# A two-layer trunk on one core: on-chip last slot groups, six query tiles, diagonal weighting in the first layer

## The chip, the cores and the metric

The kernel runs on one core of one Trainium2 chip. The metric is the device time of the whole launch in microseconds (us). The engines are TensorE (PE in the profile, its weight loads PEld), VectorE (DVE), ScalarE (ACT), GpSimd (POOL) and SyncE (SP), which issues most DMAs.

## The reference, cut to what matters

Two layers over 256 latent tokens and 256 context tokens of width 1024, in float32. A layer normalises and projects its input, runs three mixers beside each other (a long convolution, a gated recurrence called gdn, and attention with eight heads), merges them, projects, adds; then a mixture of experts adds its part:

```python
qn_l, qr_l = mla_queries(cq_l, lp)        # 8 heads: 64 plain + 32 rotary columns each
qr_l = rope_2d(qr_l, row, col)            # latent tokens only
...
x = x + (gt1 * mix).astype(x.dtype)
h2 = rms_norm(x, lp['norm2_g']) * (1.0 + sc2) + sh2
x = x + (gt2 * moe_ffn(h2, router_w, router_b, lp)).astype(x.dtype)
# moe_ffn: for each token its 2 best of 16 experts,
#   gate[:, e] * ((silu(h @ w1[e]) * (h @ w3[e])) @ w2[e]), summed
...
return rms_norm(x, final_norm_g)          # after two layers, 256 latent tokens
```

The second layer updates only the latent tokens, so its experts see 256 rows in place of 512.

## The kernel before

SBUF is an arena of 47 pages of 128 x 1024 float32, handed out in halves (`M.get`). PSUM is eight banks of 128 x 512. Work is written in two forms. *Items* are a list in a fixed order: each has weight loads on SP's queue, a preparation, products, and a post step. *Streams* are generators (a recurrence, attention, an expert's activation) that a planner (`Plan`, L267) steps in between the products of the items, by clocks that it keeps for each engine. Each engine then executes in the order in which its instructions were written. Large products are made three times from high and low parts (`mm3`, L420); `split_block` (L413) makes these parts with a ScalarE cast and a VectorE subtraction.

**Queries** (`uq_item`, L1600). Eight items a layer, one for a head. An item loads 96 columns of the weight for six row blocks. `swap` (L863) then copies the 32 rotary columns once more with halves exchanged, so that the tile has 128 columns: 64 plain, 32 rotary, 32 rotary exchanged. It is split, and 18 products follow (6 blocks x 3), over 512 token columns in layer 0 and 256 in layer 1. The post step multiplies the two rotary parts by cosines and sines out of the bank, adds, and copies the rest. The first item of a layer (`abkr_item`, L838) does the same for the one rotary key.

**Experts of layer 1** (`moe_sets`, L2208). The slots are packed in twelve groups (`NSET`) of 128 rows, each made of four runs of 32 slots of one expert. Group n goes through eight up items and, one group later, four down items. After a group's last down item its two banks are copied to a page and a GpSimd indirect DMA scatters the rows into the DRAM table `yd`, two rows a token.

**After the experts.** `overflow` (L2492) loads the largest slot count and holds a branch (L2497) that all engines pass; its body runs only when an expert has more rows than slots. Then `load_y` (L2286) reads the two rows of each token back from `yd` on SP's queue. `combine` (L2295) weighs them (ScalarE, VectorE), multiplies by the gate row (GpSimd, the last one on VectorE), adds to the residual (VectorE) and squares for the norm (ScalarE). In layer 0 that works on four token tiles of 1024 columns, in layer 1 on two tiles in halves. In layer 0 the norm of layer 1 follows and the transposes that feed its first products. In layer 1 the final norm and gain follow and the two output DMAs.

Of the kernel before, what the change touches and what calls it, by code (L numbers as in the profile page):

```python
# [28 lines left out]
D = 1024  # L29
SEQ = 256  # L30
L = 2
# [11 lines left out]
def _constants():  # L43
# [27 lines left out]
    ra, rb = np.zeros((128, SEQ)), np.zeros((128, SEQ))  # L71
    ra[32:64], ra[64:96] = c32, s32
    rb[64:96], rb[96:128] = c32, s32
    cols["ropeA"], cols["ropeB"] = ra, rb
# [287 lines left out]
LAG = (2, 1)  # L362


class Trunk:
# [209 lines left out]
    def setup(self):  # L575
# [7 lines left out]
        self.yd = [self.dr.tile([1024 >> l, D], F32, name=f"yd{l}") for l in range(L)]  # L583
        self.tokd = [self.dr.tile([512 * NE, 1], I32, name=f"tokd{l}") for l in range(L)]
# [253 lines left out]
    def abkr_item(self, l):  # L838
# [8 lines left out]
        def prep0(pg):  # L847
            self.swap(pg, 32, 64, 8)

        def post(b):  # L850
            ab, kr, t2 = self.M.get(), self.M.get(), self.M.get()
            nc.scalar.copy(ab.f()[0:16], b[0:16, :])
            ra = self.c("ropeA")
            nc.vector.tensor_tensor(kr.f()[64:96, :SEQ], b[32:64, :SEQ], ra[32:64], op=OP.mult)
            nc.vector.tensor_tensor(t2.f()[64:96, :SEQ], b[64:96, :SEQ], ra[64:96], op=OP.mult)
            nc.vector.tensor_tensor(kr.f()[64:96, :SEQ], kr.f()[64:96, :SEQ], t2.f()[64:96, :SEQ], op=OP.add)
# [4 lines left out]
        return self.win(l, 0, 512, post, "abkr", loader, prep0)  # L861

    def swap(self, pg, a, b, k):  # L863

        src = pg[:, :, a:a + 32].rearrange("p k (u s c) -> p k u s c", u=2, s=2)
        dst = pg[:, :, b:b + 32].rearrange("p k (u s c) -> p k u s c", u=2, s=2)
        for u in range(2):
            for s in range(2):
                self.nc.vector.tensor_copy(dst[:, :, u, s, :], src[:, :, u, 1 - s, :])
# [730 lines left out]
    def uq_item(self, l, h):  # L1600

        nc, M = self.nc, self.M
        nt = 512 if l < L - 1 else 256
        w = self.a["mla_w_uq"][l].rearrange("(k p) c -> p k c", p=128)

        def ld(blk):
            nc.sync.dma_start(out=blk.f(768).rearrange("p (k c) -> p k c", k=6)[:, :, 0:96], in_=w[:, :, 96 * h:96 * h + 96])

        def prep(it):
            p = it.pages[0]  # L1610
            self.swap(p.f(768).rearrange("p (k c) -> p k c", k=6), 64, 96, 6)
            it.w = self.split_block(p, 768)

        def mm(it):
# [8 lines left out]
            if h == 7:  # L1623
                for hi, lo in self.lora["q"]["x"]:
                    hi.free()
                    lo.free()

        def post(it):
            b = it.b
            q, t = M.get(), M.get()  # L1630
            rb = self.c("ropeB")
            nc.scalar.copy(q.f(nt)[0:64], b[0:64, :nt])
            nc.vector.tensor_tensor(q.f(SEQ)[64:96], b[64:96, :SEQ], rb[64:96], op=OP.mult)
            nc.vector.tensor_tensor(t.f(SEQ)[64:96], b[96:128, :SEQ], rb[96:128], op=OP.mult)
            nc.vector.tensor_tensor(q.f(SEQ)[64:96], q.f(SEQ)[64:96], t.f(SEQ)[64:96], op=OP.add)
            if nt > SEQ:
                nc.scalar.copy(q.f()[64:96, SEQ:], b[64:96, SEQ:nt])
            t.free()
            self.unbank(b)
            self.qt[h] = q  # L1640
        return Item([(2, ld)], prep, mm, post, name=f"uq{h}")
# [566 lines left out]
    def moe_sets(self, l):  # L2208
# [17 lines left out]
        def up(n, j, q):  # L2226
# [24 lines left out]
        def down(n, k):  # L2251
# [14 lines left out]
            def post(it):  # L2266
# [3 lines left out]
                y = M.get(2)  # L2270
                for hf, b in enumerate(st.pop((n, "y"))):
# [4 lines left out]
                y.free()  # L2276
            return Item([(2, ld(e)) for e in new(n)], None, mm, post, name=f"down{n}{k}", need=(f"act{n}",), moe=True)
# [6 lines left out]
        return items  # L2284

# [9 lines left out]
    def combine(self, tiles, ys, parts, after):  # L2295
# [3 lines left out]
        n = D // parts  # L2299
        units = [(t, n * i) for t in tiles for i in range(parts)]  # L2300
        ss = self.tiny(8, "css")

        def weigh(u, t, o):
            y0, y1 = ys[t, 0].f(n, o), ys[t, 1].f(n, o)
            nc.scalar.activation(y0, y0, AF.Copy, scale=self.gw[0][:, t:t + 1])
            v.scalar_tensor_tensor(y0, y1, self.gw[1][:, t:t + 1], y0, op0=OP.mult, op1=OP.add)

        def gate(u, t, o):
            y0 = ys[t, 0].f(n, o)
            (v if u == len(units) - 1 else nc.gpsimd).tensor_tensor(y0, y0, self.gt2[t // 2].f(n, o), op=OP.mult)  # L2310

        def add(u, t, o):
            x = self.xt[t].f(n, o)
            v.tensor_tensor(x, x, ys[t, 0].f(n, o), op=OP.add)

        def square(u, t, o):
            x = self.xt[t].f(n, o)
# [284 lines left out]
```

## Time and profile before

| | |
|---|---|
| time, median of 3 runs | 2086.78 us (2080.86 to 2089.03) |
| the profiled execution, its own time | 2080.96 us |
| its span, first to last instruction | 2079.3 us |
| mean granted TensorE clock | 0.94 of full speed |
| TensorE busy | 1850.6 us |
| VectorE busy | 1300.7 us |
| ScalarE busy | 873.3 us |
| GpSimd busy | 318.5 us |

Busy time is the union of an engine's instructions in the profiled execution. All helpers record their operations at one line, L210, so rows are told apart by their tiles: `pg` is a page, `bank` a PSUM bank, `cst` a constant, `yd` the table of expert rows.

### The profile page before, as it was taken

To read this page: it belongs to the slowest core of one execution; us is meant where nothing else is said; L and a number is where in the kernel's file an instruction comes from. 1 tells how busy PE (TensorE), PEld (TensorE's weight loads), DVE (VectorE), ACT (ScalarE), POOL (GpSimd) and SP (SyncE) were. 2 spreads that over 40 slices of the span, in tenths; PEclk is the share of its full clock that TensorE was granted. 3 is DMA by queue.
4 is the path that set the end of the run, shared out by engine and by line. 5 is a ranking of instruction groups with operands and counts; after the bars stand their busy time and mean duration, and the time that the engine had idled before them with its cause. 6 is when DMAs were issued, how large, how long until landed. Compare 5 with 4: busy or idle time off the path is not lost. (4 is left out here: it accounts for less than half of the span.)

```text
span 2079.3 us, 32681 instructions
## 1 busy us (share of the span) xinstructions
PE 1850.6 (89%) x12412; PEld 1369.9 (66%) x12413; DVE 1300.7 (63%) x2799; ACT 873.3 (42%) x1520; POOL 318.5 (15%) x314
## 2 busy tenths in 40 slices
PE   4899998899999989699999488998989977899993
PEld 1776786677768777588888366787768966233331
DVE  2667566654675669799999676777777755111113
ACT  3342423444434534288888444443455432111111
POOL 2212112000032204311110201131011310100002
PEclk8999999999999999799999798999989988999997
DMA  9717212412253274689998585622415529799961
GB/s 334 256 62 218 70 38 57 111 42 82 92 182 80 85 247 162 243 326 386 380 381 314 152 282 170 174 55 57 120 31 163 143 86 391 248 394 391 385 256 70
DMA packets 295184, 401.10 MB, mean 193 GB/s; under 512 B 43892, under 2 KB 185722, under 8 KB 295016
## 3 DMA queue, kind: packets, MB, share of 16 engines
q1 hardware_dynamic: 271512, 360.38, 51.5%
q0 software_dynamic: 13056, 27.15, 3.7%
q10 hardware_dynamic: 10448, 11.37, 1.7%
q8 instruction: 100, 1.64, 0.3%
q14 instruction: 68, 0.56, 0.1%
HBM read 391.94 MB, written 23.20 MB: 200 GB/s over the span
## 5 line engine op out<-in xcount | busy, mean ns | idle before, releaser
L210 PE MATMUL bank<-pg,pg 128*128 128x512 f32 (+6 forms) x10746 | 1659.6, 390 | 57.8 <-ACT pg L210 31.3
L210 PEld LDWEIGHTS bank<-pg,pg 128*128 128x128 f32 (+4 forms) x10746 | 1212.8, 167 | 455.9 <-issue 203.9
L210 DVE TENSOR_TENSOR pg<-pg,pg 128x1024 fp32r<-128x1024 f32 (+11 forms) x699 | 608.5, 903 | 157.7 <-ACT pg L210 147.8
L210 ACT CAST pg<-pg 128x1024 fp32r<-128x1024 f32 (+3 forms) x460 | 428.8, 965 | 209.7 <-DVE pg L210 139.0
L210 ACT COPY pg<-bank 64x256 f32<-64x256 f32 (+5 forms) x402 | 163.7, 440 | 285.1 <-PE bank L210 238.0
L210 PE MATMUL bank<-cst,pg 128*128 128x128 f32 (+3 forms) x935 | 142.5, 290 | 103.7 <-DVE pg L210 64.1
L210 PEld LDWEIGHTS bank<-cst,pg 128*128 128x128 f32 (+1 forms) x935 | 118.2, 159 | 147.4 <-issue 51.6
L210 POOL TENSOR_TENSOR pg<-pg,pg 128x512 f32<-128x512 f32 (+3 forms) x72 | 119.6, 1667 | 441.2 <-DVE pg L210 196.2
L210 ACT ACTIVATE pg<-bank 128x512 f32<-128x512 f32 (+1 forms) x116 | 61.0, 535 | 166.9 <-PE bank L210 156.3
L210 ACT ACTIVATE pg<-pg 128x512 f32<-128x512 f32 (+4 forms) x77 | 52.7, 692 | 146.8 <-DVE pg L210 107.1
L210 DVE SCALAR_TENSOR_TENSOR pg<-bank,vec,pg 128x510 f32<-128x510 f32 (+3 forms) x112 | 73.5, 657 | 54.6 <-ACT pg L210 52.8
L210 DVE SCALAR_TENSOR_TENSOR pg<-pg,bank 128x512 f32<-128x512 f32 (+1 forms) x92 | 54.2, 602 | 77.2 <-ACT pg L210 64.7
L210 POOL DMA_INDIRECT yd<-pg,t_vi x28 | 29.0, 1037 | 465.3 <-ACT pg L210 235.8
L210 DVE TENSOR_TENSOR pg<-bank,pg 128x512 fp32r<-128x512 f32 (+4 forms) x120 | 69.1, 596 | 27.3 <-ACT pg L210 14.6
L210 ACT CAST pg<-bank 128x512 fp32r<-128x512 f32 (+1 forms) x72 | 35.6, 517 | 100.4 <-PE bank L210 80.2
L210 DVE TENSOR_TENSOR pg<-pg,bank 128x512 f32<-128x512 f32 (+1 forms) x44 | 27.0, 613 | 80.6 <-PE bank L210 77.8
L210 POOL TENSOR_TENSOR pg<-pg 128x512 f32<-128x512 f32 (+1 forms) x12 | 14.3, 1193 | 400.0 <-ACT pg L210 348.3
L210 ACT ACTIVATE pg<-bank,t_amx,t_asq 128x512 f32<-128x512 f32 (+1 forms) x48 | 34.0, 708 | 77.4 <-DVE t_amx L210 77.4
L210 ACT ACTIVATE pg<-bank,vec 128x512 f32<-128x512 f32 (+3 forms) x64 | 41.4, 647 | 59.5 <-PE bank L210 53.6
L210 DVE COPY pg<-bank 128x512 f32<-128x512 f32 x12 | 8.3, 692 | 82.2 <-PE bank L210 75.3
L210 PE MATMUL bank<-pg,sc 128*32 128x512 f32 x384 | 53.5, 630 | 0.8 <-DMA pg<-in_w_ada_dram 0.7
L210 DVE TENSOR_REDUCE pg<-pg 128x128 f32<-128x1024 f32 (+15 forms) x128 | 43.1, 337 | 4.4
(258 smaller groups left out, 814.0 us busy)
## 6 DMA issues: line engine op xcount, KB each, us to landing
pg<-in_moe_w_dram SPq DMA_DIRECT2D x384, 512.0 KB
pg<-in_w_in_dram SPq DMA_DIRECT2D x120, 512.0 KB
pg<-in_w_ada_dram SPq DMA_DIRECT2D x96, 512.0 KB
pg<-in_w_out_dram SPq DMA_DIRECT2D x24, 512.0 KB
pg<-yd SPq DMA_DIRECT2D x12, 512.0 KB
pg<-in_mla_w_uq_dram SPq DMA_DIRECT2D x16, 288.0 KB
pg<-gcd POOLq DMA_DIRECT2D x16, 256.0 KB, 4.1
pg<-in_hy_out_dram SPq DMA_DIRECT2D x8, 512.0 KB
```

The lines of the kernel that those rows point to most:

```text
L210: return f(*a, **k)
```

## The change

Four edits.

1. Queries come from six items a layer: four of two heads' plain columns, two of four heads' rotary columns. The exchange of halves is a VectorE shuffle within 32 partitions after the product, for the key too.
2. In layer 1 the last two slot groups are not scattered. Their rows are weighted and gated out of the banks, stay in pages, and one-hot products add them to the tokens at the end (`finish`). The other ten groups' rows are read back and added by a stream (`partial`) that starts after group 9. The table is zeroed early in the layer, since rows that stay on the chip leave places in it unwritten.
3. The weights and one-hot tables for that are made when group 3 starts (`tail_weights`).
4. In layer 0 two of the four token tiles (`DIAG`) are weighted by products with diagonal matrices, and the gate multiplication of all tiles is on VectorE.

```diff
+DIAG = (1, 3)
+TAIL = (NSET - 2, NSET - 1)
+TURN = [i ^ 8 for i in range(32)]
...
-    def uq_item(self, l, h):
+    def uq_item(self, l, kind, i):
+        n, o = (64, 0) if kind == "plain" else (32, 64)
+        heads = 128 // n
         def ld(blk):
-            nc.sync.dma_start(out=blk.f(768).rearrange("p (k c) -> p k c", k=6)[:, :, 0:96], in_=w[:, :, 96 * h:96 * h + 96])
+            pg = blk.f(768).rearrange("p (k c) -> p k c", k=6)
+            for j in range(heads):
+                c = 96 * (heads * i + j) + o
+                nc.sync.dma_start(out=pg[:, :, n * j:n * j + n], in_=w[:, :, c:c + n])
...
+        def plain(it):
+            for j in range(2):
+                nc.scalar.copy(self.qt[2 * i + j].f(nt)[0:64], it.b[64 * j:64 * j + 64, :nt])
+        def rotary(it):
+            r, t = M.get(), M.get()
+            nc.scalar.copy(r.f(nt), it.b[:, :nt])
+            x, y = t.f(SEQ), t.f(SEQ, SEQ)
+            v.stream_shuffle(y, r.f(SEQ), TURN)
+            v.tensor_tensor(x, r.f(SEQ), self.c("ropeC"), op=OP.mult)
+            v.tensor_tensor(y, y, self.c("ropeS"), op=OP.mult)
+            for j in range(4):
+                q = self.qt[4 * i + j] = M.get()
+                p = slice(32 * j, 32 * j + 32)
+                v.tensor_tensor(q.f(SEQ)[64:96], x[p], y[p], op=OP.add)
+                if nt > SEQ:
+                    nc.scalar.copy(q.f()[64:96, SEQ:], r.f(nt)[p, SEQ:])
...
+                if (n, j, q) == (3, 0, 0):
+                    self.tail_weights()
...
+                if n in TAIL:
+                    for hf, b in enumerate(st.pop((n, "y"))):
+                        nc.vector.scalar_tensor_tensor(y.f(512, 512 * hf), b, self.gws[:, n - TAIL[0]:n - TAIL[0] + 1], self.gt2[0].f(512, 512 * hf), op0=OP.mult, op1=OP.mult)
+                    self.tail[n] = y
+                    return
...
+                if n == TAIL[0] - 1:
+                    self.start("partial", self.partial(l))
...
+    def zero_rows(self, l, eng):
+        z = self.M.get(2)
+        self.nc.gpsimd.memset(z.f(), 0.0)
+        for t in range(8 >> l):
+            eng.dma_start(out=self.yd[l][128 * t:128 * t + 128], in_=z.f())
...
+    def add_rows(self, l, t, eng):
+        for i, y in enumerate((y0, y1)):
+            eng.dma_start(out=y.f(), in_=src[:, i, :])
+        yield self.plan.when(y1.f())
+        x = self.xt[t].f()
+        nc.scalar.activation(y0.f(), y0.f(), AF.Copy, scale=self.gw[0][:, t:t + 1])
+        v.scalar_tensor_tensor(y0.f(), y1.f(), self.gw[1][:, t:t + 1], y0.f(), op0=OP.mult, op1=OP.add)
+        v.tensor_tensor(y0.f(), y0.f(), self.gt2[t // 2].f(), op=OP.mult)
+        v.tensor_tensor(x, x, y0.f(), op=OP.add)
+    def partial(self, l):
+        for t in range(2):
+            yield from self.add_rows(l, t, self.nc.gpsimd)
+    def finish(self, l):
+        for hf in range(2):
+            for j, n in enumerate(TAIL):
+                for t in range(2):
+                    if j == 0:
+                        bank[t] = self.bank()
+                    nc.tensor.matmul(bank[t], self.hot.f(128, 128 * (2 * j + t)), self.tail[n].f(512, 512 * hf), start=j == 0, stop=j == len(TAIL) - 1)
+            for t in range(2):
+                x = self.xt[t].f(512, 512 * hf)
+                v.tensor_tensor(x, x, bank[t], op=OP.add)
+                nc.scalar.activation(sq.f(), x, AF.Square, accum_out=ss[:, 2 * t + hf:2 * t + hf + 1])
+        v.tensor_tensor(x0, x0, self.fg.f(), op=OP.mult)
...
+        r = self.rows_rms(self.xt[:2], "fin", s2)
+        nc.scalar.activation(x0, x0, AF.Copy, scale=r[:, 0:1])
+        nc.scalar.dma_start(out=self.out[0, 0:128], in_=x0)
+        v.scalar_tensor_tensor(x1, x1, r[:, 1:2], self.fg.f(), op0=OP.mult, op1=OP.mult)
+        nc.sync.dma_start(out=self.out[0, 128:256], in_=x1)
...
+    def combine(self, ys, after):
+        for t in DIAG:
+            for hf in range(2):
+                b = bank[t, hf] = self.bank()
+                for i in range(2):
+                    nc.tensor.matmul(b, self.dg[t].f(128, 128 * i), ys[t, i].f(512, 512 * hf), start=i == 0, stop=i == 1)
+        for t in range(4):
+            if t in DIAG:
+                for hf in range(2):
+                    v.tensor_tensor(y0.f(512, o), bank[t, hf], g.f(512, o), op=OP.mult)
+                    v.tensor_tensor(x.f(512, o), x.f(512, o), y0.f(512, o), op=OP.add)
+                    nc.scalar.activation(y1.f(512, o), x.f(512, o), AF.Square, accum_out=s8[:, 2 * t + hf:2 * t + hf + 1])
+            else:
+                nc.scalar.activation(y0.f(), y0.f(), AF.Copy, scale=self.gw[0][:, t:t + 1])
+                v.scalar_tensor_tensor(y0.f(), y1.f(), self.gw[1][:, t:t + 1], y0.f(), op0=OP.mult, op1=OP.add)
+                v.tensor_tensor(y0.f(), y0.f(), g.f(), op=OP.mult)
+                v.tensor_tensor(x.f(), x.f(), y0.f(), op=OP.add)
+                nc.scalar.activation(y1.f(), x.f(), AF.Square, accum_out=ss[:, t:t + 1])
...
         items = [self.abkr_item(l)] + ([hook(self.late_setup)] if l == 0 else []) + qkv(0)
+        items += [hook(lambda: self.zero_rows(l, nc.gpsimd))] if l == L - 1 else []
...
+            self.drain(("filters",) if l < L - 1 else ("partial",))
             if l < L - 1:
+                self.diagonals()
             self.overflow(l)
```

## Rows read from the trace of the kernel before

**Rows 1.** The page: busy time, share of the span, instructions

```profile
PE 1850.6 (89%) x12412; PEld 1369.9 (66%) x12413; DVE 1300.7 (63%) x2799; ACT 873.3 (42%) x1520; POOL 318.5 (15%) x314
```

**Rows 2.** Windows: length, busy PE PEld DVE ACT POOL, clock, DMA share, GB/s

```profile
380.00:400.00 20.00, 15.95 (x64) 11.95 (x63) 13.53 (x37) 7.70 (x13) 0.00 (x0) 0.91 0.11 27
400.00:420.00 20.00, 20.00 (x86) 15.77 (x85) 13.51 (x29) 9.62 (x18) 0.00 (x0) 1.00 0.69 184
...
1420.00:1440.00 20.00, 16.61 (x191) 15.34 (x193) 15.28 (x46) 7.53 (x17) 0.00 (x0) 0.83 0.25 62
...
2020.00:2030.00 10.00, 10.00 (x100) 3.04 (x96) 0.69 (x1) 0.60 (x1) 0.01 (x1) 1.00 0.07 24
```

**Rows 3.** Timeline, TensorE in the query stages: start, us, instruction, count

```profile
402.82 9.49 PE L210 MATMUL bank<-pg,pg 128*128 128x512 f32 x39
...
1446.82 3.42 PE L210 MATMUL bank<-pg,pg 128*128 128x256 f32 x32 [0.49 <-DVE pg L210]
```

**Rows 4.** Grouped lines, VectorE, 1400 to 1462: busy us, mean ns | idle before

```profile
L210 DVE TENSOR_TENSOR pg<-pg,pg 128x768 fp32r<-128x768 f32 x8 | 7.7, 959 | 7.5 <-ACT pg L210 7.5
L210 DVE TENSOR_TENSOR pg<-bank,cst 32x256 f32<-32x256 f32 x16 | 6.8, 425 | 3.1 <-ACT pg L210 2.8
...
L210 DVE COPY pg<-pg 128x48 f32<-128x48 f32 x32 | 4.5, 205 | 0.2
...
L210 DVE TENSOR_TENSOR pg<-pg,pg 32x256 f32<-32x256 f32 x6 | 2.5, 417 | 0.2
...
L210 DVE TENSOR_TENSOR pg<-pg 32x256 f32<-32x256 f32 x2 | 0.8, 418 | 0.1
```

**Rows 5.** DMA queues, 345 to 365: packets, MB, share of 16 engines

```profile
q1 hardware_dynamic: 6277, 2.36, 45.7%
```

**Rows 6.** Timeline of the seam between the layers

```profile
1177.37 1.28 DVE L210 SCALAR_TENSOR_TENSOR pg<-pg,t_gw,pg 128x1024 f32<-128x1024 f32 x1 [14.50 <-DMA pg<-yd]
...
1180.67 1.50 DVE L210 SCALAR_TENSOR_TENSOR pg<-pg,t_gw,pg 128x1024 f32<-128x1024 f32 x1 [2.01 <-DMA pg<-yd]
...
1182.25 3.27 POOL L210 TENSOR_TENSOR pg<-pg,pg 128x1024 f32<-128x1024 f32 x1 [1.16 <-DMA pg<-yd]
1183.23 3.38 DVE L210 SCALAR_TENSOR_TENSOR pg<-pg,t_gw,pg 128x1024 f32<-128x1024 f32 x1
...
1195.77 0.17 DVE L210 TENSOR_SCALAR t_css<-t_css 128x4 f32<-128x4 f32 x1 [1.22 <-ACT pg L210]
```

**Rows 7.** Windows after two pauses of TensorE, columns as in the second group

```profile
1200.00:1205.00 5.00, 4.81 (x23) 4.81 (x24) 3.01 (x9) 1.71 (x3) 0.00 (x0) 0.50 1.19 300
...
2045.00:2050.00 5.00, 0.72 (x8) 0.00 (x0) 0.69 (x1) 0.51 (x1) 0.98 (x1) 0.83 0.12 43
```

**Rows 8.** Timeline of the end, from the last expert group's copy

```profile
2045.79 0.69 DVE L210 COPY pg<-bank 128x512 f32<-128x512 f32 x1 [6.17 <-PE bank L210]
2047.23 0.98 POOL L210 DMA_INDIRECT yd<-pg,t_vi  x1 [5.89 <-DVEq L2497]
2051.02 1.91 SPq L210 DMA_DIRECT2D pg<-yd  x4
...
2070.93 0.17 DVE L210 TENSOR_SCALAR t_finb<-t_fss 128x2 int32<-128x2 int32 x1
...
2072.95 1.15 ACT L210 ACTIVATE pg<-pg,t_finb 128x1024 f32<-128x1024 f32 x1 [4.50 <-DVE t_finb L210]
...
2074.13 0.34 ACTq L210 DMA_DIRECT2D out_dram<-pg  x1
```

**Rows 9.** Timeline, GpSimd early in layer 1

```profile
1253.93 1.04 POOL L210 TENSOR_TENSOR pg<-pg 128x512 f32<-128x512 f32 x1 [37.08 <-ACT pg L210]
```

**Rows 10.** Timeline, TensorE at 304: one full-precision product, two records

```profile
304.10 1.02 PE L210 MATMUL bank<-pg,cst 128*128 128x512 f32 x2
```

**Rows 11.** Grouped lines: that product, and VectorE out of a bank

```profile
L210 PE MATMUL bank<-pg,cst 128*128 128x512 f32 x2 | 1.0, 592 | 0.0
...
L210 DVE TENSOR_TENSOR pg<-pg,bank 128x512 f32<-128x512 f32 x2 | 1.4, 686 | 11.0 <-PE bank L210 11.0
```

More of the change, by code (lines that the diff above doesn't have):

```diff
@@ L70, in _constants @@
         s32[16 * b + 8:16 * b + 16] = np.sin(ang)
[L71 to L74, printed above, removed]
+    cols["ropeC"], cols["ropeS"] = np.tile(c32, (4, 1)), np.tile(s32, (4, 1))
     tl = np.linspace(0.0, 1.0, SEQ, dtype=np.float32)
@@ L860, in post @@
             self.start("gates", self.gdn_gates(l, ab))
[L861 to L869, printed above, removed]
+        return self.win(l, 0, 512, post, "abkr", loader)
     def gdn_gates(self, l, ab):
@@ L1622, in mm @@
                 x.free()
-            if h == 7:
+            if kind == "plain" and i == 3:
                 for hi, lo in self.lora["q"]["x"]:
@@ L2293, in load_y, with diagonals @@
         return ys
-    def combine(self, tiles, ys, parts, after):
+    def diagonals(self):
+        self.dg = {t: self.M.get() for t in DIAG}
+        for t in DIAG:
+            for i in range(2):
+                self.nc.vector.tensor_scalar(self.dg[t].f(128, 128 * i), self.c("ident"), self.gw[i][:, t:t + 1], None, op0=OP.mult)
+    def combine(self, ys, after):
         nc, M = self.nc, self.M
         v = nc.vector
[L2299 to L2317, printed above, removed]
-            nc.scalar.activation(ys[t, 1].f(n, o), x, AF.Square, accum_out=ss[:, u:u + 1])
-            if o + n == D:
-                ys[t, 0].free()
-                ys[t, 1].free()
-                self.dump(f"xout{t}", self.xt[t].f())
-                after(t)
-        for s in range(len(units) + 2):
-            for k, f in ((0, weigh), (0, gate), (1, add), (2, square)):
-                if 0 <= s - k < len(units):
-                    f(s - k, *units[s - k])
-        return ss[:, :len(units)]
@@ L2331, in layer @@
+        for t in DIAG:
+            v.tensor_tensor(ss[:, t:t + 1], s8[:, 2 * t:2 * t + 1], s8[:, 2 * t + 1:2 * t + 2], op=OP.add)
+        return ss
     def layer(self, l):
@@ L2361, in layer @@
         items += qkv(1) if at == 1 else []
-        items += [self.ukv_item(l)] + [self.uq_item(l, h) for h in range(8)]
+        items += [self.ukv_item(l)] + [self.uq_item(l, kind, i) for kind, i in (("rotary", 0), ("plain", 0), ("plain", 1), ("rotary", 1), ("plain", 2), ("plain", 3))]
         items += [hook(lambda: self.start("attend", attention()), ("loraq",))]
@@ L2448, in keep @@
                         nc.sync.dma_start(out=self.xd[128 * t:128 * t + 128], in_=self.xt[t].f())
-                ss = self.combine(range(4), ys, 1, keep)
+                ss = self.combine(ys, keep)
                 xn = self.norm_rows(self.xt[:4], "rm", ss)
@@ L2453, in build @@
             else:
[L2454 to L2467 removed]
+                self.finish(l)
             for g in self.gt2:
@@ L2512, in overflow @@
                         self.overflow_part(l, e, j)
+            if l == L - 1:
+                for t in range(2):
+                    for _ in self.add_rows(l, t, nc.sync):
+                        pass
         self.plan.off = False
```

106 lines of the change are left out of this document (66 added, 40 removed).

## The prediction

> **What bounds the kernel now.** I read the page first, then windows, the grouped lines of two stretches, and the timeline of the two places where the layers end. TensorE is busy 89% of the span [rows 1], so work taken off it counts wherever it has no idle time of its own. The windows say where that holds. In layer 0 the query stage runs from about 365 to 415 us. It has 20.00 of 20 us busy in its second half and 15.95 of 20 before it. In layer 1 the first half of the same stage (1420 to 1440) leaves 3.4 us of 20 idle, and VectorE has 15.28 us of work there [rows 2]. The expert stage of layer 1 is pure TensorE: 10.00 of 10 us, with VectorE at 0.69 and DMA at 0.07 [rows 2]. Between the layers, and after the last expert product, TensorE stands still while rows go to DRAM and back and VectorE, ScalarE and GpSimd weigh them [rows 6, 8]. So the change acts in three places, each with another limit: two query stages (TensorE and VectorE), the seam between the layers (the VectorE chain), and the end (a chain of everything).
>
> **Query tiles.** Each layer drops two of eight items, of 18 products each, so 36 products. At 512 columns 39 records take 9.49 us, 0.243 each, so 36 take 8.7. At 256 columns 32 take 3.42, 0.107 each, so 36 take 3.8 [rows 3]. TensorE loses 12.5 us. VectorE loses per layer 32 swap copies (4.5), 24 small rope operations (6.8 + 2.5 + 0.8), and two of eight low-part subtractions (1.9): 16.5 in all [rows 4]. It gains twice a shuffle, two multiplications of 256 columns and four additions. None of these ran in this shape, and I give all seven the 0.42 of the 256-column row, since partitions have not changed that price: 5.9. Net 10.6 us less per layer, on an engine that keeps TensorE waiting there. How much of the idle comes back has to be bounded: nothing, or all of 4.1 + 3.4 us of idle [rows 2]. I take 3. **Query stages: -15.5**, ends -8.7 (the wait chains of layer 1 swallow its part, see the rivals) and -20.0.
>
> The loads are cut finer: 12,288 pieces of 256 and 128 bytes in place of 6,144 of 384. At present 6,277 packets take 45.7% of 16 engines over 20 us, which is 23 ns a packet [rows 5]. At that price for every piece the loads of a layer grow from 9 to 18 us of transfer; if only bytes counted, by nothing. Either way a fourfold rotary load takes at most 3,072 x 23 / 16 = 4.4 us, and the DMA is idle for the next 40 us in both layers, so I cost it at zero; without that cover it would be up to 9 us a layer. The Trainium skill, DMA: Bandwidth & Descriptors, Specifications, speaks against this edit: below 512 bytes a transfer does not reach line rate. By it the 18 us would hold, which the idle transfer time covers too. SP issues eight more DMAs a layer at some 0.4 us, with nothing queued behind them that is due.
>
> The key part of the first item loses four copies and three small operations and gains five: zero, within half a microsecond.
>
> **Zeroing for layer 1.** GpSimd gets a memset and four DMAs after the first queries and keys, about 5 us of its time. It is idle for 37 us before 1253.93 [rows 9], and the next thing behind these in its queue is that operation on the keys of the first recurrence. Cost zero under this cover; all of it, one for one on the recurrence, if the cover were gone.
>
> **Seam between the layers.** Now: rows of tile 0 are there at 1177.37, the last sum of squares at 1195.77 [rows 6]. Of the four weighing operations the third takes 3.38 where the first took 1.28, and the fourth is like the third: GpSimd's multiplications run beside them [rows 6]. After the change GpSimd has none. Tile 0 on VectorE: 1.28 and two plain passes over as many columns (1.2 each, an estimate by the same row), done 1181.1. Tile 1 arrives at 1180.67. Its four products: the two records of one product span 1.02 us at 0.59 each, so a record starts every 0.43 and a product is 0.86 at 2.4 GHz, 1.72 at 1.2 GHz [rows 10, 11]. TensorE has been off, and the first stretch of work after this pause is granted 0.50 [rows 7], so I take 1.72. The first half is ready at 1182.6, the second at 1186.1. Two passes of 0.69 on it [rows 11]: 1187.5. Then ScalarE must square (0.8 for half a tile, taken between half and all of its 1.15 for a whole one [rows 8]) before it scales tile 2 (1.15), because its queue is in order, and VectorE waits: 1189.5. Tile 2: 1193.2. Tile 3, whose products are ready by then: four passes of 0.69, 1195.95. Square 0.8, two tiny additions 0.35: 1197.1, against 1195.77. **Seam: +1.3.** With full-clock products the same walk ends at 1194.4 (-1.4); with later rows +3. So the diagonals cost what the relief from GpSimd gives.
>
> **The end.** Now 33.6 us lie between the last product (2045.7) and the end of the span, 2079.3. The chain [rows 8]: copy, scatter at 2047.23, the engines leaving the overflow branch together when the scatter has landed, reads from 2051.02, weighing until the inverse root starts at 2070.93, scaling at 2072.95, output issued at 2074.13, 5.2 us more until it has landed. After: the branch is still there, so the final products wait for it. Without a scatter in flight I estimate 1.7 us after the last multiplication (2046.5), so 2048.2; ends 0.75 (the step from copy to scatter [rows 8]) and 4.5 (the wait as now). Eight products: 6.9 us at full clock, 13.8 at half. The clock falls in just such a pause: 0.83 on average over 2045 to 2050, of which TensorE worked 0.72 us [rows 7]. I take three products at half and five at full, 9.4 us: 2057.6. Addition 0.7, gain 1.2 (the square lies beside it), sum and inverse root 2.4 [rows 8], scaling 1.3, output 5.2: 2068.4. **End: -10.9**, ends -14.3 and -3.6.
>
> The partial weighing of the ten earlier groups is costed at nothing. It starts when group 9 is done, some 26 us before the last product. Its reads, scalings and sums use DMA, ScalarE and VectorE, which are nearly idle there (2020 to 2030 in [rows 2]). The weights and one-hot tables are made seven groups earlier, on GpSimd, which holds only gathers needed two groups later.
>
> **Sum.** -15.5 + 1.3 - 10.9 = -25.1. Against the profiled execution's own 2080.96 (span 2079.3): 2055.9. That execution stands 5.8 under the median of the runs (2086.78), so a median would be up to 2061.7. I predict 2059, between the two.
>
> **Rivals.**
> - *The query stages give nothing.* For it: layer 1's idle time [rows 2]; the second recurrence starts only after the first, a chain of small steps. Against it: 20.00 of 20 us in layer 0. Seam and end alone are -9.6: 2071 to 2077. Chance 0.10.
> - *VectorE was the real limit there.* All idle comes back, the seam and the end go at full clock: -20.0 - 1.4 - 14.3 = -35.7, so 2045 to 2051. Chance 0.12.
> - *The final products run at 1.2 GHz throughout.* For it: 4.81 of 5 us busy after a pause and still 0.50 [rows 7]. 4.4 us more: 2060 to 2066. The Trainium skill, TensorE: Matmul & The Clock Gate, has the throttled state as the default that activity releases; by it the first products at least are slow, as the rows show. Chance 0.14, inside the range.
> - *The partial weighing is late,* so that the change does not do what it says. If its steps are emitted only when the list of products is empty, reads (4 us) and two tiles at 3.7 on VectorE stand ahead of the branch: +11, net -14, 2067 to 2073. Against it: 26 us of room. Chance 0.08.
> - *The planner orders the rest worse.* Every later instruction is placed by its clocks, so stretches that the diff leaves alone move too. Layer 1 has 3.4 us idle of 20 in one stretch [rows 2]; three such stretches more would be 10 us, nine 30: 2069 to 2090. Nothing in the profile speaks for it or against it. Chance 0.08.
> - *Slower: the four zeroing writes hold GpSimd.* If they keep its queue until they have landed, the first recurrence of layer 1 starts late, and the second after it, one for one. At 5 us nothing happens; from 1253.93 on each microsecond is one. To cancel 25.1 the hold must last to about 1279, more than 35 us for 2 MB; beyond that the kernel is slower. Price 2082 to 2100. Chance 0.04.
>
> **How the numbers follow.** The forecast itself (2051 to 2067) has 0.44, and the predicted time is its middle, 2059. The range is 2045 to 2076: it leaves out the slow rival, three quarters of the one before it and the far end of the first, 0.13 together. About 0.5% (10 us) is what a measurement of this kernel tells from no change, so the border lies at 2076.3. Faster: 0.44 + 0.12 + 0.14 + 0.08, with 0.07 of the first rival and 0.02 of the planner's: 0.87. Same: what is left of these two, 0.09. Slower 0.04.
>
> **What would show it.** Right: the query stage of a layer has 108 products in place of 144; a layer boundary some 8 to 11 us earlier; the query stage of layer 1 another 4 to 7 shorter; the last sum of squares of the seam about 20 us after the first read lands, with the weighing at 1.28 and no GpSimd multiplications; from the last expert product to the end 23 us in place of 33.6, with eight products in two groups behind the branch. Wrong: the boundary of layer 1 no earlier though the products are gone; a GpSimd operation on the keys that waits for the zeroing; weighing of earlier groups after the last expert product; more idle TensorE in stretches that the diff does not touch, because the planner's order moved.

## The result, and the profile after

The changed kernel takes 2054.69 us (median of 4 runs, 2051.80 to 2056.84) against 2087.23 us before on the same chip (4 runs, 2080.86 to 2089.03): a ratio of 0.9849, 95% interval 0.9824 to 0.9873. The profiled execution took 2055.86 us, with a span of 2053.8 against 2079.3, so 25.5 us less. The prediction was 2059 (2045 to 2076) with 0.87 on faster; the sum behind it was -25.1 from span to span. The medians lie 32.5 us apart: the profiled execution of before is among the fastest of its runs, that of the changed kernel among the slower.

The page shows TensorE about as busy as before, in a shorter span (72 query products went, 16 full-precision ones of 17.8 us together came at the seam and the end), and 20 us less VectorE work [rows 1]:

```profile
PE 1852.8 (90%) x12372; PEld 1363.4 (66%) x12373; DVE 1280.5 (62%) x2732; ACT 869.3 (42%) x1520; POOL 306.7 (15%) x320
```

The timeline of TensorE in the query stage of layer 0, first a line of before, then the changed kernel with its window [rows 2, 3]: the pauses before the products are for ScalarE and VectorE, none is for the finer loads. The pause of 3.47 us that before had in the middle is gone, and 380 to 400 is now full.

```profile
387.63 0.74 PE L210 MATMUL bank<-pg,pg 128*128 128x512 f32 x2 [3.47 <-ACT pg L210]
...
367.76 0.73 PE L207 MATMUL bank<-pg,pg 128*128 128x512 f32 x2 [1.59 <-ACT pg L207]
368.75 20.17 PE L207 MATMUL bank<-pg,pg 128*128 128x512 f32 x84 [0.26 <-DVE pg L207]
...
380.00:400.00 20.00, 20.00 (x90) 15.89 (x89) 15.10 (x40) 11.57 (x19) 0.00 (x0) 1.00 0.83 226
```

The timeline of the seam, VectorE and then TensorE [rows 6]: the two weighings left on VectorE (tiles 0 and 2) take 1.28 to 1.29, that of tile 2 no longer 3.38; tile 2 waits 1.89 us for ScalarE, as the walk had it; the last sum comes 19.16 us after the first weighing starts (18.40 before).

```profile
1168.46 1.29 DVE L207 SCALAR_TENSOR_TENSOR pg<-pg,t_gw,pg 128x1024 f32<-128x1024 f32 x1 [13.70 <-ACT pg L207]
...
1175.10 0.69 DVE L207 TENSOR_TENSOR pg<-bank,pg 128x512 f32<-128x512 f32 x1 [2.83 <-DMA pg<-yd]
...
1180.12 1.28 DVE L207 SCALAR_TENSOR_TENSOR pg<-pg,t_gw,pg 128x1024 f32<-128x1024 f32 x1 [1.89 <-ACT pg L207]
...
1187.62 0.17 DVE L207 TENSOR_SCALAR t_css<-t_css 128x4 f32<-128x4 f32 x1
...
1171.43 6.21 PE L207 MATMUL bank<-pg,pg 128*128 128x512 f32 x10 [14.89 <-DMA pg<-yd]
1178.02 2.81 PE L207 MATMUL bank<-pg,pg 128*128 128x512 f32 x6 [0.38 <-DMA pg<-yd]
```

Thirty microseconds later stands a wait that the prediction did not have. The timeline of SP's queue and of ScalarE: the two writes of `xd`, written in the code right after the first two tiles' sums, are issued at 1208.20, 27 issues after the last read of `yd`, behind the loads of the next layer's weights; ScalarE waits 4.85 us until one has landed, because it is given that page to write. The gates of layer 1 (`t_beta`) are made 31.9 us after the seam's last sum, before 28.5. The writes are no later than they were: 20.6 us after the last sum, before 21.3 (1217.1). What is new is who gets the page; e_old_seam below shows it.

```profile
1167.48 16.80 SPq L207 DMA_DIRECT2D pg<-in_w_in_dram  x8
...
1202.90 5.21 SPq L207 DMA_DIRECT2D pg<-in_w_ada_dram  x2
1208.20 0.87 SPq L207 DMA_DIRECT2D xd<-pg  x2
...
1217.09 1.05 ACT L207 CAST pg<-pg 128x1024 fp32r<-128x1024 f32 x1 [4.85 <-DMA xd<-pg]
1219.54 0.20 ACT L207 ACTIVATE t_beta<-bank 128x32 f32<-128x32 f32 x1 [1.39 <-DVE t_gt L207]
```

GpSimd's timeline where the zeros are written [rows 9]: four issues of 2.25 us together, behind the squares that were at stake, not ahead of them. The next operation (1261.40) starts when `t_grs` is there, 11.60 us after the first square; before, 11.61 (1253.93 to 1265.54).

```profile
1252.68 0.95 POOL L207 MEMSET pg<- 128x1024 f32 x1
1253.93 2.25 POOL L207 DMA_DIRECT2D yd<-pg  x4 [0.30 <-POOL pg L207]
1261.40 2.03 POOL L207 TENSOR_TENSOR pg<-pg,t_grs 128x512 f32<-128x512 f32 x2 [5.21 <-issue]
```

The timeline of the end [rows 8]: TensorE's last expert products, in before and then in the changed kernel, and behind them VectorE, TensorE, ScalarE and the output of the changed kernel. The earlier groups' rows are weighed by 2026.3, 5.5 us before the last group's (2031.80); the eight products take 8.80 us behind the branch; the span ends 5.0 us after the output's first issue. From the last expert product (2032.59) to the end are 21.2 us; before, 33.6 (from 2045.72).

```profile
2034.81 10.91 PE L210 MATMUL bank<-pg,pg 128*32 128x512 f32 x100
...
2025.54 7.05 PE L207 MATMUL bank<-pg,pg 128*32 128x512 f32 x64
...
2023.83 2.48 DVE L207 TENSOR_TENSOR pg<-pg,pg 128x1024 f32<-128x1024 f32 x2
...
2031.80 1.61 DVE L207 SCALAR_TENSOR_TENSOR pg<-bank,t_gws,pg 128x512 f32<-128x512 f32 x2 [4.16 <-PE bank L207]
2039.10 0.69 DVE L207 TENSOR_TENSOR pg<-pg,bank 128x512 f32<-128x512 f32 x1 [5.69 <-PE bank L207]
...
2043.39 0.69 DVE L207 TENSOR_TENSOR pg<-pg,bank 128x512 f32<-128x512 f32 x1 [0.17 <-PE bank L207]
...
2034.55 8.80 PE L207 MATMUL bank<-pg,pg 128*128 128x512 f32 x16 [1.97 <-PEq L2589]
...
2047.62 1.15 ACT L207 ACTIVATE pg<-pg,t_finb 128x1024 f32<-128x1024 f32 x1 [2.79 <-DVE t_finb L207]
2048.80 0.37 ACTq L207 DMA_DIRECT2D out_dram<-pg  x1
```

To compare many kernels I cut each profiled span at the same six instructions of its timeline: the low-rank queries' statistics of layer 0 and 1 (`t_lqa`, ahead of the query stage), the last scatter of layer 0, the first operation of the norm on the seam's sums (`t_css`), the gates (`t_beta`) and the scatter of the tenth group of layer 1. The stretch up to the first cut is 350 to 353 us in all of them. Times in us; the last column is the median of the runs with its lowest and highest.

| kernel | layer 0 from queries | to `t_css` | to gates | to layer 1's queries | to tenth scatter | to the end | median |
|---|---|---|---|---|---|---|---|
| before | 815.2 | 29.5 | 28.5 | 179.9 | 614.9 | 60.3 | 2087.23 (2080.9 to 2089.0) |
| changed | 806.2 | 30.2 | 31.9 | 181.2 | 605.2 | 47.9 | 2054.69 (2051.8 to 2056.8) |
| e_old_queries | 818.3 | 30.4 | 30.3 | 179.9 | 616.1 | 44.8 | 2073.02 (2068.4 to 2076.7) |
| e_heads | 815.6 | 29.8 | 31.1 | 178.6 | 615.6 | 45.2 | 2071.32 (2068.1 to 2072.4) |
| e_old_seam | 802.1 | 29.5 | 27.5 | 178.8 | 606.2 | 45.1 | 2046.97 (2042.3 to 2049.7) |
| e_scatter_all | 803.9 | 30.6 | 31.0 | 177.0 | 607.8 | 62.6 | 2067.40 (2065.5 to 2069.4) |
| e_after_again | 806.0 | 29.9 | 31.4 | 177.1 | 606.8 | 45.7 | 2051.81 (2050.3 to 2054.6) |
| e_keep_pool | 802.4 | 30.0 | 27.4 | 178.6 | 609.2 | 46.3 | 2045.28 (2043.5 to 2048.5) |
| e_scale_first | 804.4 | 28.7 | 27.8 | 178.3 | 605.6 | 45.9 | 2046.94 (2042.8 to 2047.7) |
| e_old_seam_pool | 803.9 | 29.7 | 27.5 | 178.7 | 607.4 | 45.5 | 2046.28 (2045.5 to 2053.3) |
| e_both | 802.4 | 28.1 | 27.4 | 179.3 | 607.2 | 45.9 | 2045.54 (2042.7 to 2047.8) |
| e_both_early | 803.9 | 28.6 | 27.3 | 178.6 | 605.1 | 46.4 | 2046.99 (2041.5 to 2048.7) |
| e_no_diagonals | 802.2 | 27.2 | 27.3 | 177.3 | 606.8 | 45.5 | 2043.36 (2041.2 to 2045.3) |
| e_double_products | 804.6 | 30.6 | 31.1 | 178.9 | 606.0 | 52.8 | 2057.22 (2055.8 to 2057.7) |

Row two minus row one: -9.0, +0.7, +3.4, +1.3, -9.7, -12.4, and +0.2 ahead of the first cut: -25.5. Equal code differs by 2 to 4 us from one profile to the next in the long columns, so single rows are read to no better than that. Before has one profile only.

### The profile page after: what moved, and what is told of

Same layout as the page of the kernel before. It is cut to its first block, busy times and chain, and to the rows that moved or that the text cites. A ratio compares the mean times of both kernels' runs of the same rounds, so it can differ in the third digit from the quotient of the medians.

```text
span 2053.8 us, 32569 instructions
## 1 busy us (share of the span) xinstructions
PE 1852.8 (90%) x12372; PEld 1363.4 (66%) x12373; DVE 1280.5 (62%) x2732; ACT 869.3 (42%) x1520; POOL 306.7 (15%) x320
## 5 line engine op out<-in xcount | busy, mean ns | idle before, releaser
L207 PE MATMUL bank<-pg,pg 128*128 128x512 f32 (+7 forms) x10712 | 1662.2, 391 | 66.1 <-DVE pg L207 23.9
L207 PEld LDWEIGHTS bank<-pg,pg 128*128 128x128 f32 (+5 forms) x10712 | 1207.2, 167 | 468.5 <-issue 223.9
L207 DVE TENSOR_TENSOR pg<-pg,pg 128x1024 fp32r<-128x1024 f32 (+12 forms) x687 | 600.4, 907 | 159.2 <-ACT pg L207 152.5
L207 ACT CAST pg<-pg 128x1024 fp32r<-128x1024 f32 (+2 forms) x456 | 424.5, 967 | 192.7 <-DVE pg L207 129.5
L207 ACT COPY pg<-bank 64x256 f32<-64x256 f32 (+4 forms) x398 | 162.8, 441 | 278.6 <-PE bank L207 254.4
L207 POOL TENSOR_TENSOR pg<-pg,pg 128x256 f32<-128x256 f32 (+3 forms) x62 | 97.0, 1567 | 406.1 <-ACT pg L207 180.7
L207 DVE TENSOR_TENSOR pg<-pg,bank 128x512 f32<-128x512 f32 (+1 forms) x48 | 29.7, 619 | 91.4 <-PE bank L207 88.6
(270 smaller groups left out, 802.2 us busy)
```

What stands on the lines that cost most here:

```text
L207: return f(*a, **k)
```

## The experiments

All are edits of the changed kernel. The first four shared one chip, the next four another, the last four a third. Before's own median on these three was 2085.9, 2087.8 and 2083.1 us, so medians from different chips are compared to no better than some 5 us; every ratio is to before on the same chip. The unedited kernel was run again on the second chip only (e_after_again, called its second measurement).

**e_old_queries**: the former `uq_item`, with the sines and cosines taken from the new tables.

```
-[self.uq_item(l, kind, i) for kind, i in (("rotary", 0), ("plain", 0), ...)]
+[self.uq_item(l, h) for h in range(8)]
```

> The changed kernel with the queries as they were before: eight items of one head each, 144 products a layer, the rotated columns copied beside the others by 24 small VectorE copies a head group. Theory (the query stages' products pay, in both layers): 15.5 to 19 us slower than the changed kernel; the last scatter of layer 0 comes 8 to 10 us later, and the query stage of layer 1 gives 4 to 10 us more. Rival 1 (layer 1's larger gain was not the queries', but another order of the rest): 9 to 13 us slower, with layer 1 giving 4 or less. Rival 2 (the wait for the write of xd at the start of layer 1 comes from the queries ending earlier): that wait, 4.85 us in the changed kernel, is gone here too. If it stays, it belongs to the seam.

Measured: ratio to before 0.9938 (0.9916 to 0.9959); 18.3 us over the changed kernel's median, 21.2 over that of its second measurement below, both on other chips. Layer 0 from the queries is 818.3, layer 1 616.1, both as before within the spread. So the query stages pay in both layers, at or over the upper end of the theory. ScalarE's wait for `xd` stays (3.52 us here), so rival 2 falls: the wait is not the queries' doing.

**e_heads**: eight items, no rotated copies.

```
-self.swap(p.f(768).rearrange("p (k c) -> p k c", k=6), 64, 96, 6)
-it.w = self.split_block(p, 768)
+it.w = self.split_block(it.pages[0], 576)
...
-self.mm3(it.b[:, :nt], it.w[0].r(128, 128 * k), ...
+self.mm3(it.b[0:96, :nt], it.w[0].r(96, 96 * k), ...
```

> Eight query items of one head each with 144 products a layer as before, but of 96 rows, without the copies of rotated columns: the rotation is done by a shuffle and three VectorE operations after the products, and fewer elements are split. It takes the copies and the quarter of the split off VectorE and leaves TensorE's number of products alone. Theory (the number of products pays): within 4 us of the kernel with old queries, so 12 to 19 us slower than the changed kernel. Rival (VectorE's copies and splits set the pace of the stage): within 4 us of the changed kernel.

Measured: 0.9943 (0.9922 to 0.9963), 1.7 us under e_old_queries. The windows of layer 1 from `t_lqa` to the first attention head's scaling, in before, the changed kernel and this one (columns as in [rows 2]):

```profile
1404.00:1463.30 59.30, 50.04 (x469) 44.24 (x469) 46.33 (x129) 22.31 (x46) 6.84 (x10) 0.92 0.35 89
```

```profile
1400.80:1450.40 49.60, 42.98 (x420) 37.70 (x419) 36.62 (x88) 21.36 (x44) 6.56 (x10) 0.94 0.41 97
```

```profile
1405.70:1466.30 60.60, 53.58 (x493) 47.21 (x492) 46.55 (x126) 21.34 (x48) 7.07 (x10) 0.92 0.29 78
```

The changed kernel has 9.7 us less between these points: 7.06 less TensorE work and 2.64 less idle. The grouped lines of TensorE in the first two windows give the part of the query products alone: 6.2 us for 36 products.

```profile
L210 PE MATMUL bank<-pg,pg 128*128 128x256 f32 x144 | 23.2, 317 | 5.5 <-ACT pg L210 4.8 <-DVE pg L210 0.7
```

```profile
L207 PE MATMUL bank<-pg,pg 128*128 128x256 f32 x108 | 17.0, 308 | 6.6 <-ACT pg L207 5.3 <-DVE pg L207 1.3
```

In e_heads TensorE has 53.58 us of work again, also because the planner put more other work there (493 records for 469), and the layer ends no earlier than before (615.6). TensorE's idle in the window is smaller here too, 7.02 us for 9.26, but it does not shorten the layer. The number of products pays; VectorE's copies, by themselves, bring 1.7 us at most, with runs that overlap those of e_old_queries.

**e_old_seam**: the former weighing between the layers.

```
-                self.diagonals()
...
-                ss = self.combine(ys, keep)
+                ss = self.combine_old(range(4), ys, 1, keep)
```

> The changed kernel with the old weighing between the layers: no diagonals on TensorE, the gates on GpSimd for three of four tiles, all sums on VectorE. Theory (the new seam costs 0.8 us up to its last sum, and by the late write of xd a further 2 to 4 us at the start of layer 1): 2 to 4 us faster than the changed kernel, and ScalarE's wait of 4.85 us for the write of xd is gone. Rival 1 (the new seam's price is only its 0.8 us, the rest of the loss at layer 1's start comes from the planner): 0 to 1 us faster, the wait stays. Rival 2 (the new seam gains, as it is meant to): 1 to 4 us slower.

Measured: 0.9828 (0.9807 to 0.9849); its median is 7.7 us under the changed kernel's first and 4.8 under its second, on other chips, and by the ratios it is 4.4 and 1.5. Up to `t_css` 29.5, to the gates 27.5: together 5.1 us less than in the changed kernel's first profile and 4.3 less than in its second, and nobody waits for `xd`. The theory holds in kind, with a price in the trace somewhat over the 2 to 4 that I gave. But it is not the late write that makes the wait. The view of `xd`, in before and here (least, middle and greatest time of an issue in ns, first and last start in us):

```profile
L210 SPq DMA_DIRECT2D xd<-pg x2: 386/429/472, 1217.1 to 1217.7; - x2
```

```profile
L207 SPq DMA_DIRECT2D xd<-pg x2: 382/383/384, 1202.8 to 1203.3; - x2
```

The old seam has its writes 21.3 and 21.1 us after `t_css`, the changed kernel 20.6. What differs is the page: in the program of the changed kernel ScalarE's cast ahead of the gates writes the page that the first write of `xd` reads; in before and here it writes another, and the page of `xd` is next written only behind the gates. Over all profiles, the six with this wait (3.5 to 4.9 us) have 30.3 to 31.9 us to the gates, the eight without it 27.3 to 28.5.

**e_scatter_all**: the last two groups scattered, the former end.

```
-                if n in TAIL:
-                    ...  # weighed into self.tail
...
-                self.finish(l)
+                ys = self.load_y(l, 2)
+                ss = self.combine_old((0, 1), ys, 2, lambda t: None)
```

> The changed kernel with the old end: the last two groups are scattered like the others, all rows are read back after the last scatter, weighed and added, then normed; nothing is weighed early. The zeroing of yd stays. Theory (the end is worth what the traces show, 33.6 against 21.2 us after the last expert product): 11 to 13 us slower, and everything up to the last expert product within 1 us. Rival (part of the end's gain is paid for by the partial weighing and the tail's weights earlier in the experts' stage): under 10 us slower, with the last expert product 2 us or more earlier than in the changed kernel.

Measured: 0.9924 (0.9902 to 0.9945), 12.7 us over the changed kernel. Its stretch from the tenth scatter is 62.6 us against 44.8 to 47.9 in the kernels with the new end and eight products, and in its timeline VectorE stands still for the rows on their way through DRAM (behind the last expert product this end takes 35.9 us, 2.3 more than in before, so the edit prices the new end that much too high):

```profile
2028.80 0.69 DVE L207 COPY pg<-bank 128x512 f32<-128x512 f32 x1 [6.17 <-PE bank L207]
2042.15 1.41 DVE L207 SCALAR_TENSOR_TENSOR pg<-pg,t_gw,pg 128x512 f32<-128x512 f32 x2 [12.67 <-DMA pg<-yd]
```

The experts' stretch up to the tenth scatter (607.8) is no shorter than with the tail's weights, and from there to the last expert product, where the partial weighing runs, are 26.68 us here as in the changed kernel and in before. So both are hidden, and the rival falls.

**e_after_again**: no edit.

> The changed kernel itself, unedited, beside the three edits of its seam that share its chip. Both theories: the median of the changed kernel, 2054.7 us, within 3; its profile says how much the stages vary from one execution to the next. If the eight products at its end again start at the low clock, the end takes about 21 us after the last expert product; in the kernels with old queries, with 96-row heads and with the old seam it took about 18 to 19 after the first weighing of the last group.

Measured: 0.9835 (0.9810 to 0.9860). The wait for `xd` is there again, 4.36 us. The end is not: TensorE and the windows of the first products behind the branch, here and in the first profile of the same kernel:

```profile
2032.62 7.11 PE L207 MATMUL bank<-pg,pg 128*128 128x512 f32 x16 [1.48 <-PEq L2589]
...
2032.60:2037.00 4.40, 4.38 (x11) 2.01 (x12) 1.30 (x2) 0.72 (x2) 0.00 (x0) 1.00 0.02 6
```

```profile
2034.50:2039.00 4.50, 4.45 (x7) 1.94 (x8) 0.00 (x0) 0.00 (x0) 0.00 (x0) 0.62 0.01 4
```

Seven records in 4.45 us at a granted 0.62, or eleven in 4.38 at 1.00. In nine of the ten profiles with this end and eight products TensorE took 7.10 to 7.27 us for them, once 8.80. So the profile of the result, with 47.9 us in the last column, is the exception.

**e_keep_pool**

```
-nc.sync.dma_start(out=self.xd[...], in_=self.xt[t].f())
+nc.gpsimd.dma_start(out=self.xd[...], in_=self.xt[t].f())
```

> The changed kernel with the two writes of xd issued from GpSimd's queue in place of SP's, where they stand behind weight loads. Theory (ScalarE's wait of 3.5 to 4.9 us at the start of layer 1 is for this write alone): the wait is gone and the gates of layer 1 come 2 to 4 us sooner after the seam's last sum, the kernel is 2 to 4 us faster than the changed kernel on the same chip. Rival (the wait only moves: the engines wait there for the weights next, whose loads the writes no longer hold back): within 1 us.

Measured: 0.9800 (0.9776 to 0.9824), 6.5 us under the changed kernel on the same chip; the runs do not overlap. The timeline of GpSimd's queue and of ScalarE: the writes go out at 1170.28 and 1176.12, 15 and 9 us ahead of `t_css` in place of 20 us after it, and the gates come 4.0 us sooner after `t_css` (27.4 for 31.4).

```profile
1170.28 0.61 POOL L207 DMA_DIRECT2D xd<-pg  x1 [8.27 <-DVE pg L207]
1176.12 0.59 POOL L207 DMA_DIRECT2D xd<-pg  x1 [5.24 <-DVE pg L207]
...
1212.57 0.20 ACT L207 ACTIVATE t_beta<-bank 128x32 f32<-128x32 f32 x1 [2.03 <-DVE t_gt L207]
```

The theory holds for the wait; of the 6.5 us the trace places 4.0, as forecast, the rest is within the spread of the other columns. The Trainium skill, DMA: Bandwidth & Descriptors, Issuing engines are not separate DMA queues, says that starting DMAs on several engines saves only the time that the sequencer takes to start them, usually small beside the DMA itself. Here it was not small: on SP the writes stood behind 27 loads whose issues filled 40 us.

**e_scale_first**

```
         for t in range(4):
+            if t not in DIAG:
+                nc.scalar.activation(ys[t, 0].f(), ys[t, 0].f(), AF.Copy, scale=self.gw[0][:, t:t + 1])
+        for t in range(4):
...
-                nc.scalar.activation(y0.f(), y0.f(), AF.Copy, scale=self.gw[0][:, t:t + 1])
```

> The changed kernel with ScalarE's two scalings of the seam issued ahead of the squares of the tile before. Theory (VectorE waits 1.9 us for ScalarE's scaling of tile 2, behind tile 1's squares): the last sum of the seam comes 1 to 2 us sooner after the first read lands, the kernel 1 to 2 us faster. Rival (the reads from yd set the time of the seam): less than 0.5 us.

Measured: 0.9805 (0.9780 to 0.9830), 4.9 us under the changed kernel. To `t_css` 28.7 for 29.9: the 1.2 us of the theory. The other 3.6 are in the next column, and nobody waits for `xd` although the writes go out as late as ever, 21.4 us after `t_css`:

```profile
1205.93 0.88 SPq L207 DMA_DIRECT2D xd<-pg  x2
...
1212.28 0.20 ACT L207 ACTIVATE t_beta<-bank 128x32 f32<-128x32 f32 x1 [2.07 <-DVE t_gt L207]
```

So there are two ways out of that wait: an earlier write, or another page for the cast. This edit, meant for something else, did the second: in its program the cast ahead of the gates writes a page that no write of `xd` reads.

**e_old_seam_pool**: both lines of e_old_seam and that of e_keep_pool.

> The changed kernel with the old seam (gates on GpSimd, no diagonals) and with the writes of xd on GpSimd's queue. Theory (the old seam already has no wait for that write): within 1.5 us of the kernel with the old seam, so 4 to 8 us faster than the changed kernel. Rival (the writes on SP hold back weight loads behind them, seen or not): a further 2 us faster. Another (GpSimd issues them behind its gates, and its descriptors cost time): 1 to 3 us slower than with the old seam alone.

Measured: 0.9817 (0.9790 to 0.9843), 5.5 us under the changed kernel on the same chip and 0.7 under e_old_seam on another. The theory holds as far as two chips can be compared: without the wait there is nothing to see of a gain from the queue.

**e_both**: e_keep_pool and e_scale_first.

> The two seam edits together: the writes of xd on GpSimd's queue, and the scalings issued ahead of the squares. Each alone was 5 to 6.5 us faster than the changed kernel beside it, and in each ScalarE's wait for xd is gone. Theory (they remove the same wait, and the scalings bring 1.2 us more at the last sum): 1 to 2 us faster than with the writes moved alone, 2043.5 to 2045. Rival (they are two gains that add up): 4 to 6 us faster than either, 2039 to 2041.

Measured: 0.9820 (0.9796 to 0.9844), 0.3 us over e_keep_pool on another chip. The stretches are 28.1 and 27.4: the scalings' gain stands in the trace, the wait is not saved twice. The rival falls; in the median the scalings' part does not show.

**e_both_early**: e_both, and

```
+                if (n, k) == (TAIL[1], 2):
+                    self.tb = {(hf, t): self.bank() for hf in range(2) for t in range(2)}
+                    self.tail_products(0)   # the four products of the group before the last
```

> Both seam edits, and the four products of the group before the last go ahead of the branch, into the last group's products (four banks hold the sums open). Theory (at the end a product is worth 0.82 us at the full clock and 1.1 or more where the clock is lower, and the experts' stage, 22.5 us a group, has room for four more): 3 to 5 us faster than the two seam edits alone; the products behind the branch take 3.3 to 4.4 us in place of 6.6 to 8.8. Rival (TensorE sets the pace of the experts' stage): the last group comes 3.3 us later and the time stays within 1 us.

Measured: 0.9823 (0.9798 to 0.9848), 1.5 us over e_both. TensorE's last timeline rows, here and in e_both:

```profile
2007.82 15.99 PE L207 MATMUL bank<-pg,pg 128*32 128x512 f32 x120
2025.45 3.67 PE L207 MATMUL bank<-pg,pg 128*128 128x512 f32 x8 [1.63 <-PEq L2595]
```

```profile
2011.12 12.22 PE L207 MATMUL bank<-pg,pg 128*32 128x512 f32 x112
2024.80 7.11 PE L207 MATMUL bank<-pg,pg 128*128 128x512 f32 x16 [1.46 <-PEq L2591]
```

It has 3.44 us less behind the branch and 3.77 more ahead of it, and the runs of the two overlap. My theory fell, and the prediction's own row had said it: TensorE is full in the experts' stage [rows 2].

**e_no_diagonals**: e_both with `DIAG = ()`.

> Both seam edits, and no tile weighed on TensorE: all four are scaled by ScalarE and weighed, gated and added by VectorE in operations of 1024 elements. Theory (VectorE's work sets the later half of the seam: a tile by diagonals costs it 2.75 us, the other way 3.76): the last sum comes 1 to 2.5 us later, the kernel 1 to 2.5 us slower than with the two seam edits alone. Rival 1 (the reads from yd set the pace, and VectorE has the room): within 0.7 us. Rival 2 (TensorE's fp32 products with TensorE's low clock hold the first tile up by more than they take off VectorE): up to 2 us faster.

Measured: 0.9808 (0.9785 to 0.9831), 2.2 us under e_both, with runs that overlap. The last sum comes 0.9 us earlier (27.2), not later: VectorE works from 1165.14 to 1180.08 with no pause, where in e_both, the same order with diagonals, it stands 2.23 and 0.78 us for the products of tile 1:

```profile
1171.76 0.69 DVE L207 TENSOR_TENSOR pg<-bank,pg 128x512 f32<-128x512 f32 x1 [2.23 <-PE bank L207]
...
1173.95 0.69 DVE L207 TENSOR_TENSOR pg<-bank,pg 128x512 f32<-128x512 f32 x1 [0.78 <-PE bank L207]
```

The theory falls; the sign is rival 2's, the size is not settled.

**e_double_products**

```
-nc.tensor.matmul(bank[t], self.hot..., start=j == 0, stop=j == len(TAIL) - 1)
+for r in range(2):
+    nc.tensor.matmul(bank[t], self.hot..., start=j == r == 0, stop=j == len(TAIL) - 1 and r == 1)
```

> The changed kernel with the eight products at the end done twice into the same sums, so that the last two groups' rows are added twice to the output. It prices a product behind the branch. Theory (they run at the full clock but for the first after the pause): the products take 6.6 to 7.1 us more and the kernel is 6 to 8 us slower than the changed kernel. Rival (half the clock through all of them): 13 us more.

Measured: 0.9873 (0.9846 to 0.9900); 2.5 us over the first median of the changed kernel, 5.4 over the second, on other chips, so the medians do not show the 6 to 8. The trace does: the end is 7.1 us longer than in e_after_again (52.8 for 45.7), and TensorE's row gives 0.87 us a product at a granted 1.00 (2.4 GHz). The rival falls.

```profile
2031.49 13.97 PE L207 MATMUL bank<-pg,pg 128*128 128x512 f32 x32 [1.83 <-PEq L2590]
```

## Why the prediction was right

**Query stages** (-15.5 predicted). The mechanism is right, the term too small: -9.0 and -9.7, so -18.7, in the first profile. Over all profiles the eleven with six tiles have 802 to 806 and 605 to 609 us in the two layers, the three with eight items 815 to 818 and 615 to 616: some 12 and 9 less. Two terms were mis-sized. One is the price of layer 1's products: 3.8 us at 0.107 each, from a stretch at full clock [rows 3]. The 144 products before took 23.2 us, 0.161 each, and dropping 36 took off 6.2; the stage begins below full clock (0.83 granted from 1420 to 1440 [rows 2]). The other is the share of 3 us of idle for both layers: in layer 0 the 4 us between 380 and 400 came back whole, in layer 1 2.6 us. What set that idle free is not settled: it is smaller in e_heads too.

**Finer loads, key part, zeroing, partial weighing** (0). As predicted. The finer loads take 74.4% of the 16 DMA engines from 345 to 365 where the old ones took 45.7% [rows 5], but the pauses of TensorE ahead of the query products are for ScalarE and VectorE. The recurrence starts as before, though for another reason than given: the zeroing stands behind its squares and not ahead of them. e_scatter_all has the experts' stage no shorter.

**Seam** (+1.3). The walk holds to half a microsecond at its own end: +0.8 measured, with the predicted wait for ScalarE (1.89 us) and weighings of 1.28. The products were at a granted 0.50 to 0.55 in their first 3.6 us only, not in all of tile 1; the second half was ready when the walk had it (8.4 us after the first weighing's start, 8.7 in the walk). The step that failed is that it stopped at the last sum. A changed order of work hands the pages out in another order, and the page that the late write of `xd` reads went to the cast ahead of the gates; this cost 3.4 us more. With e_keep_pool, e_scale_first and e_old_seam that is shown. Relief from GpSimd is real for the weighing: 1.28 for 3.38. The Trainium skill, SBUF — State Buffer, SBUF: two separate sides, has a lock there: a VectorE operation with two inputs in SBUF and a GpSimd operation that reads SBUF share a port pair, which the first to start holds for its whole instruction. The trace agrees: 3.38 us beside a GpSimd multiplication [rows 6], 1.28 in every weighing of e_no_diagonals, where GpSimd multiplies nothing. The waits for tile 1 (2.83 us, which the profile puts down to a read; 2.23 in e_both, put down to the diagonals' products) and for ScalarE gave the relief back; without diagonals, in e_no_diagonals, the last sum came 0.9 us earlier than in e_both.

**End** (-10.9). Measured -12.4, and -14.6 in the second profile; the others with this end and eight products have about as much (44.8 to 46.3 in the last column). From the last expert product to the first one behind the branch it was 1.97 and 1.48 us where the sum had 2.5 (2045.7 to 2048.2); the products took 8.80 and 7.11 where it had 9.4 with three of eight at half the clock. So the term was mis-sized by the slow products: the far end, all at full clock, is what came in eleven of twelve profiles. The rival of products at 1.2 GHz throughout did not come in any.

Of the other rivals, the one with no gain from the query stages, the late partial weighing and the zeroing fell. The one that made VectorE the real limit is wrong in its reason (e_heads) but near in two of its sizes, -20.0 for the queries and -14.3 for the end. The planner's order did turn worse in one place, the page of `xd`, by 3 to 4 us instead of 10 to 30. From span to span the errors, -3.2, +2.8 and -1.5, with 1.5 in stretches that I had at nothing, nearly cancel: the total was better than its terms. That it met the measured -25.5 is luck: the errors cancel, and the two profiled executions stand at opposite ends of their runs. By medians the change is 32.5 us, and 36.0 on the chip of e_after_again, so the sum was 7 to 11 us short, by its queries and its end.

## What to carry to other kernels

When an edit changes the order of work, follow also the writes out of pages that will be reused: ask which queue issues them, what stands ahead there, and who gets the page next. A late write costs nothing until somebody is given its page; a one-word change of queue was worth more here than the reworked weighing. Where an engine is full, as TensorE in the experts' stage, moving work from the tail into it changes nothing, and removing products pays at least their own time, at the clock of the stretch they stood in. Test each part of a bundled change by itself: the bundle was 1.5% faster, and one of its three parts, the seam, cost 4 to 5 us in the trace. Set medians beside medians: a sum that agrees with one pair of profiles may owe it to the pair.

## What the runs showed of the hardware that was not expected

The same kernel came out of TensorE's pause at the branch with a granted clock of 0.62 over 4.5 us in one execution (pause 1.97 us) and of 1.00 in another (1.48 us). Of twelve profiles with such a pause of 0.48 to 1.97 us only that one was slow; it had the longest pause, and one of 1.89 us was followed by 1.00. Whether those 0.08 us or chance decided is open; the price was 1.7 us (8.80 for 7.11). And SP's queue took from 0.4 to 5.5 us for one issue of a 512 KB load (eight in 16.80 us, two in 5.21), so that a write 27 issues down started 40 us after the first of them.
